# Value products as float32 column halves in runs of eight, unsplit q and k in two of four attention groups, and one VectorE step in a third

## The chip, the cores and the metric

The kernel runs on one core of one Trainium2 chip. The metric is the device time of one execution in microseconds; 2697.52 us is the median of three runs before the change. The core's engines are named as in the profile: PE is TensorE (matmuls; PEld its weight loads), DVE is VectorE, ACT is ScalarE, POOL is GpSimd and SP is the engine whose queue issues nearly all DMAs.

## The reference

The reference is a bidirectional encoder trunk of two layers over 1024 tokens and 1024 features, float32 throughout:

```
for l in range(DEPTH):                                   # 2 layers
    h = rms_norm(x, norm1_g[l])
    proj = h @ w_in[l]                                   # columns of four head groups
    (a_cq, a_ckv, a_kr, b_q, b_k, b_v, c_q, c_k, c_v, d_q, d_k, d_v) = jnp.split(proj, splits, axis=-1)
    y_a = mla_mixer(...)      # A: 4 heads, latent q and k of 64 + 32, values of 64, dense
    y_b = diff_mixer(...)     # B: 4 heads, two softmaxes of 32 each: w = p[0] - lam * p[1], values of 64, dense
    y_c = swa_mixer(...)      # C: 4 q heads on 2 kv heads of 64, +-128 window with a sink logit
    y_d = na_mixer(...)       # D: 4 heads of 64, neighbourhood on the 64-wide grid with a bias
    mix = jnp.concatenate([rms_norm(y_a, ...), y_b, rms_norm(y_c, ...), rms_norm(y_d, ...)], axis=-1)
    x = x + mix @ w_out[l]
    h = rms_norm(x, norm2_g[l])
    x = x + jnp.square(jax.nn.relu(h @ w_up[l])) @ w_down[l]
return rms_norm(x, final_norm_g)
```

## The kernel before

Everything lies with features on the partitions and tokens on the free axis. A float32 operand of a matmul is split into a high and a low part in the type float32r (`split`, L192: ACT copies the high part, DVE or POOL subtracts it to get the low one), and a product is then made of float32r matmuls on these parts. For the projections there are three such passes (`passes`, L219). The MLP works with seven products of half blocks in place of eight.

Each layer runs its attention groups in the order B, D, C, A. `weave` (L545) takes one step of an attention group at a time and puts in steps of other work, the *fill*: the latent projections and D's projections beside B, C's projections and the latent up-projections beside D, the first part of the output projection beside C and A. The framework then schedules the instructions of each engine by a planner of its own, in which priority and estimated times count, so that the order on PE is not the order of the code.

Every projection result goes through DRAM on its way to attention. It is evacuated with its norm or rotary factors, split into two parts (`emit_parts`, L582; `to_parts`, L629; `to_values`, L635) and stored; the attention group loads it back into stacked tiles of 128 partitions. In D, for each head, q's high part and low part lie one above the other in one tile, k's high part lies twice in a second tile, and k's low part twice in a third (L1045 to L1050), and two float32r matmuls with a contraction of 128 rows give the scores. C does the same. The values of a head are 128 columns wide: 64 of the high part and 64 of the low part.

In the dense groups B and A (`dense`, L818) four steps per group of two query tiles each make four PE transpositions of the probabilities into one PSUM bank (`step`, L842), ACT and DVE split them into `pth` and `ptl`, and one step later PE multiplies them with the values (`product`, L826): four float32r matmuls of 256 columns a step, sixteen per group. The upper and the lower 64 output rows are added in `pv_out` (L749). B makes its combined probabilities with a scaled copy on ACT (L898) and an addition on POOL (through L190).

In the banded groups D and C (`banded`, L966) one block of 128 queries sees up to three blocks of 128 keys. `score` (L973) makes a block's scores, `finish` reduces, adds mask or bias and exponentiates, `parts` (L986) transposes and splits, `apply` (L998) multiplies with the values. One head is worked at a time, with scores four blocks ahead. The row sums' reciprocals are sent through DRAM to be spread over the partitions (`denominators`, L761; `rows_of`, L269; `spread`, L284).

Of the kernel before, what the change touches and what calls it, by code (L numbers as in the profile page):

```python
# [21 lines left out]
P = 128  # L22
# [78 lines left out]
def layout(i):  # L101

    def padded(a, axis):
# [9 lines left out]
    wo = i["w_out"].reshape(n, 8, P, DM)[:, [2, 3, 6, 7, 4, 5, 0, 1]].reshape(n, DM, DM)  # L113
# [23 lines left out]
        + [col(i["out_g_" + s]) for s in ("mla", "swa", "na")]  # L137
# [10 lines left out]
class Trunk:  # L148
    def __init__(self, ctx, tc, d, out):
        self.ctx, self.tc, self.nc, self.d, self.out = ctx, tc, tc.nc, d, out  # L150
        self.ahead, self.tails = 4, deque()
        pool = lambda **k: ctx.enter_context(tc.tile_pool(**k))
        self.const = pool(name="const", bufs=1)
        self.xp = pool(name="xp", bufs=8)
        self.big = pool(name="big", bufs=16)
        self.wp = pool(name="wp", bufs=3)
        self.cp = pool(name="cols", bufs=2)
        self.dram = pool(name="dram", bufs=1, space=bass.MemoryType.DRAM)
# [110 lines left out]
    def rows_of(self, col, grid=False):  # L269
# [7 lines left out]
        if grid:  # L277
            flat = dr.rearrange("a b -> (a b)").rearrange("(r b c) -> b r c", r=16, b=8)
            self.store(flat, sb.rearrange("b (r c) -> b r c", r=16))
        else:  # L280
            self.store(dr, sb)
# [99 lines left out]
    def attention(self, l):  # L381
# [8 lines left out]
        qb, kb, vb = dr([2, 2, 4, 16, 2, S], "qb"), dr([2, 2, 4, 16, 2, S], "kb"), dr([4, P, 8, P], "vb")  # L390
        qd, kd, vd = dr([2, 2, P, S], "qd"), dr([2, 2, P, S], "kd"), dr([4, P, 8, P], "vd")
        qc, kc, vc = dr([2, 2, 2, 32, 2, S], "qc"), dr([2, 2, 32, 2, S], "kc"), dr([2, P, 8, P], "vc")
        lat, krd = dr([2, 3, P, S], "lat"), dr([2, 16, 2, S], "krd")
        qa = dr([2, 2, P, S], "qan"), dr([2, 4, 16, 2, S], "qar")
        ka, va = dr([2, 2, P, S], "kan"), dr([4, P, 8, P], "va")
# [13 lines left out]
        def proj_d():  # L409
            for t in range(2):  # L410
                yield from one(T_DQ[t], xs, self.ev_grid(rb, self.to_parts(qd[:, t], 0.125)))
                yield from one(T_DK[t], xs, self.ev_grid(rb, self.to_parts(kd[:, t])))
                yield from one(T_DV[t], xs, self.ev_grid(rb, self.to_values(vd[2 * t:2 * t + 2])))

        def proj_c():
            tabs = self.table("64", rb, nc.gpsimd)
            for t in range(2):
                yield from one(T_CQ2[t], xs, self.ev_rope(tabs, qc[:, t]))
            yield from one(T_CK, xs, self.ev_rope(tabs, kc))
# [4 lines left out]
        with ExitStack() as stack, ExitStack() as att:  # L424
            self.ap = att.enter_context(sbuf("att"))
            with self.banks(mm=2, tr=2, sb=3, pv=1):
                with sbuf("proj", "right") as self.pp:
# [37 lines left out]
                    self.weave(self.attn_d(l, qd, kd, vd, y["d"]), fill, self.RD, self.LD, every=self.EV[1])  # L465
                gout = lambda n: self.gout[n][:, l]
# [123 lines left out]
    def ev_rope(self, tabs, dst):  # L590

        dst = dst.rearrange("a g f h s -> a (g f) h s")

        def ev(n, ps):
# [7 lines left out]
            self.emit_parts(t1, [(dst[:, :, h, sl].rearrange("a p s -> p a s"), slice(h * 64, h * 64 + 64))  # L602
                                 for h in range(2)])
# [30 lines left out]

    def to_values(self, dst, tag="mm"):  # L635
# [3 lines left out]
        def then(n, y):  # L639
# [3 lines left out]
            src = ps.rearrange("p (k h d) -> p h k d", k=4, h=2)  # L643
            b = self.both()
            v = b.rearrange("p h (k e) -> p h k e", k=4)
            nc.scalar.activation(v[..., 0:64], src, AF.Copy)
            self.tt(v[..., 64:128], src, v.bitcast(F)[..., 0:64], ALU.subtract)
            self.keep(dst[:, :, n * 4:n * 4 + 4].rearrange("h p k e -> p h (k e)"), b.bitcast(F))
# [100 lines left out]
    def pv_out(self, pv, y, j, half, grid=False):  # L749

        t = self.ap.tile([P, 512], R, tag="ptl", bufs=3, name="pvt").bitcast(F)[0:64]
        self.nc.scalar.activation(t, pv[64:128], AF.Copy)
        a, b, o = pv[0:64], t, y[j * 64:(j + 1) * 64]
        if grid:
            a, b = (v.rearrange("p (b r c) -> p b r c", b=4, r=16) for v in (a, b))
            o = o.rearrange("p (r b c) -> p b r c", b=8, c=8)[:, 4 * half:4 * half + 4]
        else:
            o = o[:, half * 512:half * 512 + 512]
        self.tt(o, a, b, ALU.add)

    def denominators(self, z, dst, grid=False):  # L761
        r = self.col("rz", 8)
# [3 lines left out]
        self.spread(dst, rows)  # L766
# [26 lines left out]
    def vtile(self, src):  # L793
        v = self.ap.tile([P, 8, P], R, tag="v", bufs=2, name="v")
        self.load(v.bitcast(F), src)
# [22 lines left out]
    def dense(self, heads):  # L818
# [5 lines left out]
        ready = []  # L824

        def product(job, j, h, lo):  # L826
            probs, g, v, y, half, done = job
            if g % 2 == 0 and j == 0:
                self.pv = self.bank("pv")
            out = self.pv[:, (g % 2) * 256:(g % 2) * 256 + 256]  # L830
            for k in range(2):
                kt = j * 2 + k
                sl = slice(k * 256, k * 256 + 256)
                nc.tensor.matmul(out, v[:, kt], h[:, sl], start=kt == 0, stop=False)  # L834
                nc.tensor.matmul(out, v[:, kt], lo[:, sl], start=False, stop=kt == 7)  # L835
            if j == 3:
                if g % 2:
                    self.pv_out(self.pv, y, half, g // 2)
                if g == 3:
                    done()  # L840

        def step(job, j):  # L842
# [5 lines left out]
            h, lo = self.transposed(512)  # L848
            self.split(h, lo, t)
            ready.append((job, j, h, lo))  # L850
            if len(ready) > 1:
                product(*ready.pop(0))
# [15 lines left out]
        product(*ready.pop(0))  # L868
        yield True

    def attn_b(self, l, t, qb, kb, vb, out):
# [3 lines left out]
        def head(h2):  # L875
# [15 lines left out]
            def probs(qt):  # L891
# [6 lines left out]
                nc.scalar.activation(ps[1], ps[1], AF.Copy, scale=c)  # L898
                self.tt(ps[0], ps[0], ps[1], ALU.add, nc.gpsimd)
# [66 lines left out]
    def banded(self, qs, ks, v, y, j, finish, grid=False):  # L966
# [4 lines left out]
        tiles, pair = {}, {}  # L971

        def score(i):  # L973
            if i % 2 == 0:
                pair["p"] = self.ptile()
            at = i % 2 * 512
            lo, hi = max(i - 1, 0), min(i + 1, 7)
            keys = slice(lo * P, (hi + 1) * P)
            s0, w = at + (lo - i + 1) * P, (hi - lo + 1) * P
            ps = self.bank("sb")[:, :w]  # L980
            for n, k in enumerate(ks):
                mm(ps, qs[:, i * P:(i + 1) * P], k[:, keys], start=n == 0, stop=n == 1)
            tiles[i] = pair["p"][:, at:at + 384]
            finish(ps, pair["p"][:, s0:s0 + w], i)

        def parts(kb):  # L986

            t = self.bank("tr")
            i0, i1 = max(kb - 1, 0), min(kb + 1, 7)
            for i in range(i0, i1 + 1):  # L990
                nc.tensor.transpose(t[:, (i - i0) * P:(i - i0 + 1) * P],
                                    tiles[i][:, (kb - i + 1) * P:(kb - i + 2) * P], self.ident)
            w = (i1 - i0 + 1) * P
            h, l = self.transposed(w)
            self.split(h, l, t[:, :w])
            return h, l, i0, i1

        def apply(pv, half, kb, part):  # L998
            h, l, i0, i1 = part
            q0, q1 = max(i0, half * 4), min(i1, half * 4 + 3) + 1  # L1000
            src = slice((q0 - i0) * P, (q1 - i0) * P)
            dst = pv[:, (q0 - half * 4) * P:(q1 - half * 4) * P]
            mm(dst, v[:, kb], h[:, src], start=False, stop=False)
            mm(dst, v[:, kb], l[:, src], start=False, stop=kb == 4 + 3 * half)
# [4 lines left out]
        pv = self.zeroed()  # L1009
        held = []  # L1010
        for kb in range(8):
            if kb + self.ahead < 8:
                score(kb + self.ahead)
            part = parts(kb)
            if kb in (3, 4):
                held.append(part)
            if kb <= 4:
                apply(pv, 0, kb, part)
            else:
                apply(pv, 1, kb, part)  # L1020
            if kb == 4:
                self.pv_out(pv, y, j, 0, grid)
                pv = self.zeroed()
                for i, p in enumerate(held):
                    apply(pv, 1, 3 + i, p)
            yield True
        self.pv_out(pv, y, j, 1, grid)

    def zeroed(self):

        pv = self.bank("pv")
        self.nc.tensor.matmul(pv, self.zero, self.zero[:, 0:1].broadcast_to([P, 512]), start=True, stop=False)
        return pv

    def attn_d(self, l, qd, kd, vd, ys):
        nc = self.nc
        for t in range(2):
            y, rz = self.ypair(), self.rz_tile()
            for h2 in range(2):
                h = 2 * t + h2  # L1040
                bias = self.ap.tile([P, 6, P], F, tag="bias", bufs=1, name="bias")
                self.load(bias, self.d["bias"][l, h])
                qs, ks = self.stack(), [self.stack() for _ in range(2)]
                rows = slice(h2 * 64, (h2 + 1) * 64)
# [454 lines left out]
```

## Time and profile before

| | us |
|---|---|
| median of three runs (2692.25 to 2699.81) | 2697.52 |
| profiled execution | 2692.41 |
| its span on the core | 2690.6 |
| PE, sum of matmul times (95% of the span) | 2545.8 |
| DVE busy (75%) | 2014.2 |
| ACT busy (54%) | 1442.9 |
| POOL busy (18%) | 496.9 |

The granted TensorE clock was 0.971 on average. The DMA engines moved 389.15 MB. In the first layer B runs from about 85 to 330 us, D to 415, C to 480, A to 630, the rest of the output projection to 705 and the MLP to 1350; in the second B starts at about 1414, D at 1651, C at 1735, A at 1804, and A ends at 1960. In the profile's rows a group is given by line, engine, operation, the tile written and the tiles read; then come count, busy time, the mean time of one in ns, and the engine's idle time before them with what ended it. A line is often that of a helper, such as L190 for any two-operand step and L196 for any rounded copy.

### The profile page before, as it was taken

How to read it: one execution, taken by the hardware profiler on the slowest of the kernel's cores; microseconds unless marked ns; L12 is line 12 of the kernel's file. 1: busy time of each engine (PE TensorE's matmuls, PEld its weight loads, DVE VectorE, ACT ScalarE, POOL GpSimd, SP SyncE). 2: the span in 40 equal slices, each digit the busy share in tenths (PEclk: the TensorE clock that was granted, in tenths of full speed). 3: DMA queues.
4: the chain of work that ended last, by engine and by line, in shares of the span. 5: the costliest groups of instructions: out<-in, count | busy, mean ns of one | idle time of the engine just before them, and what ended most of it. 6: DMA issues, size and time to landing. Idle time of an engine off the chain costs nothing.

```text
span 2690.6 us, 36835 instructions
## 1 busy us (share of the span) xinstructions
PE 2545.8 (95%) x12296; PEld 2107.6 (78%) x12296; DVE 2014.2 (75%) x3827; ACT 1442.9 (54%) x2601; POOL 496.9 (18%) x306
## 2 busy tenths in 40 slices
PE   8989988999899999999999999789998999999997
PEld 7778876787778887888877788678887788778886
DVE  6777867774977778888668777677749677788886
ACT  4667757664534444444437777576635344444444
POOL 2555642201000000000035556331010000000000
PEclk9999989999999999999999999889999999999998
DMA  5533598322144447444244446962221444664431
GB/s 169 177 106 123 160 282 254 83 88 60 51 154 143 161 162 269 146 141 141 96 136 140 121 118 174 306 200 70 70 71 61 152 152 151 227 221 150 132 102 63
DMA packets 186927, 389.15 MB, mean 145 GB/s; under 512 B 23712, under 2 KB 26736, under 8 KB 186736
## 3 DMA queue, kind: packets, MB, share of 16 engines
q1 hardware_dynamic: 172912, 361.62, 43.7%
q10 hardware_dynamic: 13824, 25.17, 2.6%
q8 instruction: 97, 1.59, 0.2%
q14 instruction: 94, 0.77, 0.1%
HBM read 263.29 MB, written 123.41 MB: 144 GB/s over the span
## 4 chain that ended last, share of the span: by engine, by line
PE 74%; DVE 12%; DMA 6%; ACT 4%; issue 3%; POOL 1%; SPq 0%; DVEq 0%; ACTq 0%; POOLq 0%
PE u L222 8%; PE u L224 8%; PE u L223 8%; PE mm L222 5%; PE mm L223 5%; PE mm L224 5%; PE p L222 5%; PE p L223 5%; PE p L224 5%; PE sb L810 3%; PE tr L846 2%; DVE p L812 2%; DVE part L190 2%; PE pv L835 2%; PE pv L834 2%
## 5 line engine op out<-in xcount | busy, mean ns | idle before, releaser
L196 ACT ACTIVATE wh<-raw 128x512 fp32r<-128x512 f32 x448 | 281.8, 630 | 595.9 <-PE u L223 336.0
L190 DVE TENSOR_TENSOR wl<-raw,wh 128x512 fp32r<-128x512 f32 x448 | 306.8, 685 | 76.9 <-ACT wh L196 75.6
L190 POOL TENSOR_TENSOR wl<-ws,wh 128x512 fp32r<-128x512 f32 (+1 forms) x112 | 146.5, 1310 | 1107.0 <-DMA saved<-x 664.1
L224 PE MATMUL u<-far,wl 128*128 128x512 f32 x768 | 302.4, 394 | 6.2 <-DVE wl L190 6.0
L222 PE MATMUL u<-far,wh 128*128 128x512 f32 x768 | 302.4, 394 | 3.3 <-ACT ev L1251 2.1
L223 PE MATMUL u<-far,wh 128*128 128x512 f32 x768 | 301.8, 393 | 0.9 <-DVE far L190 0.9
L190 DVE TENSOR_TENSOR ptl<-tr,pth 128x512 fp32r<-128x512 f32 (+2 forms) x384 | 238.3, 629 | 67.5 <-ACT pth L196 65.8
L815 ACT ACTIVATE p<-p,nm 128x1024 f32<-128x1024 f32 x192 | 220.1, 1147 | 91.1 <-DVE nm L812 89.6
L196 ACT ACTIVATE pth<-tr 128x512 fp32r<-128x512 f32 (+2 forms) x384 | 204.9, 546 | 104.4 <-PE tr L846 55.8
L222 PE MATMUL p<-far,wh 128*128 128x512 f32 x640 | 251.2, 393 | 2.6 <-DVE ev L190 2.6
L224 PE MATMUL p<-far,wl 128*128 128x512 f32 x640 | 250.0, 391 | 2.9 <-DVE wl L190 2.9
L223 PE MATMUL p<-far,wh 128*128 128x512 f32 x640 | 250.3, 391 | 0.0
L810 PE MATMUL sb<-stack 96*128 96x512 f32 x640 | 217.6, 421 | 18.8 <-DVE nm L812 17.8
L190 POOL TENSOR_TENSOR p<-p 128x1024 f32<-128x1024 f32 x64 | 154.0, 2410 | 141.4 <-ACT p L898 132.1
L190 DVE TENSOR_TENSOR raw<-raw 128x512 f32<-128x512 f32 x256 | 174.6, 686 | 6.7 <-DMA raw<-in_w_up 2.0
L224 PEld LDWEIGHTS u<-far,wl 128*128 128x128 f32 x768 | 145.8, 190 | 38.4 <-DVE wl L190 7.9
L222 PEld LDWEIGHTS u<-far,wh 128*128 128x128 f32 x768 | 146.1, 190 | 35.3 <-ACT ev L1251 2.9
L223 PEld LDWEIGHTS u<-far,wh 128*128 128x128 f32 x768 | 145.8, 190 | 31.9 <-DVE far L190 1.6
L222 PE MATMUL mm<-xh,wh 128*128 128x512 f32 x416 | 168.9, 406 | 1.3 <-DVE part L190 0.7
L812 DVE CUSTOM_DVE_ANT_0 p<-sb,zero,nm 128x512 f32<-128x512 f32 x192 | 142.4, 742 | 32.2 <-PE sb L810 28.6
L224 PE MATMUL mm<-xh,wl 128*128 128x512 f32 x416 | 166.5, 400 | 0.0
L223 PE MATMUL mm<-xl,wh 128*128 128x512 f32 x416 | 166.4, 400 | 0.0
(245 smaller groups left out, 5993.1 us busy)
## 6 DMA issues: line engine op xcount, KB each, us to landing
act<-acts SPq DMA_DIRECT2D x224, 256.0 KB
raw<-in_w_up SPq DMA_DIRECT2D x128, 256.0 KB
acts<-ev SPq DMA_DIRECT2D x128, 256.0 KB
raw<-in_w_down SPq DMA_DIRECT2D x128, 256.0 KB
acts<-ev ACTq DMA_DIRECT2D x96, 256.0 KB
ws<-in_w_in SPq DMA_DIRECT2D x76, 256.0 KB
rz<-drows SPq DMA_DIRECT2D x40, 256.0 KB
stack<-kd SPq DMA_DIRECT2D x32, 256.0 KB
```

Of the source, the lines that this page charges most:

```text
L190: (eng or self.nc.vector).tensor_tensor(out=out, in0=a, in1=b, op=op)
L196: nc.scalar.activation(hi, src, AF.Copy)
L222: mm(ps, w[0], x[0][:, sl], start=start, stop=False)
L223: mm(ps, w[0], x[1][:, sl], start=False, stop=False)
L224: mm(ps, w[1], x[0][:, sl], start=False, stop=stop)
L810: self.nc.tensor.matmul(ps, q[:, qt * P:(qt + 1) * P], k[:, sl], start=i == 0, stop=i == len(passes) - 1)
L812: self.nc.vector.tensor_tensor_reduce(out=p[:, sl], in0=ps, in1=self.zero[:, 0:1].bitcast(F).broadcast_to([P, 512]), scale=-scale, scalar= ...
L815: self.nc.scalar.activation(p, p, AF.Exp, bias=nm[:, 1:2], scale=-1.0, accum_out=z)
L834: nc.tensor.matmul(out, v[:, kt], h[:, sl], start=kt == 0, stop=False)
L835: nc.tensor.matmul(out, v[:, kt], lo[:, sl], start=False, stop=kt == 7)
L846: nc.tensor.transpose(t[:, k * 256 + i * P:k * 256 + (i + 1) * P], p[:, (j * 2 + k) * P:(j * 2 + k + 1) * P], self.ident)
```

## The change

- Value products (A, B, C, D): the transposed probabilities are copied once in float32 (`pt`), by ACT in B and D, by DVE and ACT in turn in C and A. The values are float32 and 64 columns wide. In A and B two successive key tiles go to PSUM partitions 0 to 63 and 64 to 127, in a run of eight matmuls per group, issued two steps into the next group; `pv_out` adds the two halves as before. In C and D the two halves are two heads, so nothing is added (`pair_out`).
- Scores of D and C: q and k are stored and loaded as they are, two heads in one tile of 128 partitions, and the score of a head is one float32 matmul with a contraction of the 64 rows of its half. The two heads of a pair are worked together, with scores three blocks ahead. In C a pair is the two kv heads with the same q index, and the rows of the output weights and of the gain are reordered for it. Bias and mask lie in tiles of the pool of `stack` (L743).
- B: the two exponentiated tiles are combined by one VectorE instruction in place of the copy on ACT and the addition on POOL.

The core of the diff:

```diff
-        self.ahead, self.tails = 4, deque()
+        self.ahead, self.tails = 3, deque()
...
-                yield from one(T_DQ[t], xs, self.ev_grid(rb, self.to_parts(qd[:, t], 0.125)))
-                yield from one(T_DK[t], xs, self.ev_grid(rb, self.to_parts(kd[:, t])))
+                yield from one(T_DQ[t], xs, self.ev_grid(rb, self.to_rows(qd[t], 0.125)))
+                yield from one(T_DK[t], xs, self.ev_grid(rb, self.to_rows(kd[t])))
...
+            self.turns = (False, False)
...
+                self.turns = (True, False)
...
+    def to_rows(self, dst, scale=None):
+
+        def then(n, y):
+            if scale is not None:
+                self.nc.scalar.activation(y, y, AF.Copy, scale=scale)
+            self.keep(dst[:, n * 512:n * 512 + 512], y)
+        return then
...
-    def transposed(self, w):
-
-        return [self.ap.tile([P, 512], R, tag=n, bufs=3, name=n)[:, :w] for n in ("pth", "ptl")]
+    def transposed(self, ps):
+
+        t = self.ap.tile([P, 512], F, tag="pt", bufs=self.NT, name="pt")[:, :ps.shape[1]]
+        if self.turns[0]:
+            self.nc.vector.tensor_copy(t, ps)
+        else:
+            self.nc.scalar.activation(t, ps, AF.Copy)
+        self.turns = self.turns[::-1]
+        return t
...
+        def products():
+            job, pts = runs.pop(0)
+            probs, g, v, y, half, done = job
+            if g % 2 == 0:
+                self.pv = self.bank("pv")
+            out = self.pv[:, (g % 2) * 256:(g % 2) * 256 + 256]
+            for n, j in enumerate((3, 2, 1, 0)):
+                for k in range(2):
+                    nc.tensor.matmul(out[k * 64:(k + 1) * 64], v[:, j * 2 + k], pts[j][:, k * 256:k * 256 + 256],
+                                     start=n == 0, stop=n == 3)
...
                     if job:
                         step(job, 2 * i)
                         step(job, 2 * i + 1)
+                    if i == 0 and runs:
+                        products()
...
-                nc.scalar.activation(ps[1], ps[1], AF.Copy, scale=c)
-                self.tt(ps[0], ps[0], ps[1], ALU.add, nc.gpsimd)
+                nc.vector.scalar_tensor_tensor(out=ps[0], in0=ps[1], scalar=c, in1=ps[0], op0=ALU.mult, op1=ALU.add)
...
-            for n, k in enumerate(ks):
-                mm(ps, qs[:, i * P:(i + 1) * P], k[:, keys], start=n == 0, stop=n == 1)
+            ps = [self.bank("sb")[:, :w] for _ in heads]
+            for b, r in zip(ps, heads):
+                mm(b, q[r, i * P:(i + 1) * P], k[r, lo * P:(hi + 1) * P], start=True, stop=True)
...
+        def products(pv, half, kbs):
+            for kb in kbs:
+                pts, i0, i1 = done[kb]
+                q0, q1 = max(i0, half * 4), min(i1, half * 4 + 3) + 1
+                for r, v, pt in zip(heads, vs, pts):
+                    mm(pv[r, (q0 - half * 4) * P:(q1 - half * 4) * P], v[:, kb], pt[:, (q0 - i0) * P:(q1 - i0) * P],
+                       start=False, stop=kb == 2 + 3 * half)
```

More of the change, by code (lines that the diff above doesn't have):

```diff
@@ L765, in denominators @@
         yield
-        self.spread(dst, rows)
+        for j in range(n):
+            self.spread(dst[j * 64:(j + 1) * 64] if n > 1 else dst, rows, j, n)
         yield
@@ L823, in dense @@
         nc = self.nc
[L824 to L840, printed above, removed]
+        ready, runs = [], []
         def step(job, j):
@@ L847, in step @@
                                         p[:, (j * 2 + k) * P:(j * 2 + k + 1) * P], self.ident)
[L848 to L852, printed above, removed]
+            ready.append(self.transposed(t))
+            if j == 3:
+                runs.append((job, list(ready)))
+                ready.clear()
+        def products():
[8 more added lines that the diff above has]
+                                     start=n == 0, stop=n == 3)
+            if g % 2:
+                self.pv_out(self.pv, y, half, g // 2)
+            if g == 3:
+                done()
         job = None
@@ L867, in dense @@
             step(job, j)
-        product(*ready.pop(0))
+        while runs:
+            products()
         yield True
@@ L986, in parts @@
         def parts(kb):
-            t = self.bank("tr")
             i0, i1 = max(kb - 1, 0), min(kb + 1, 7)
[L990 to L1004, printed above, removed]
+            out = []
@@ new lines, in parts, with zeroed @@
+            for j in range(2):
+                t = self.bank("tr")
+                for i in range(i0, i1 + 1):
+                    at = j * 512 + (kb - i + 1) * P
+                    nc.tensor.transpose(t[:, (i - i0) * P:(i - i0 + 1) * P], tiles[i][:, at:at + P], self.ident)
+                out.append(self.transposed(t[:, :(i1 - i0 + 1) * P]))
+            done[kb] = out, i0, i1
+        def zeroed():
+            pv = self.bank("pv")
+            mm(pv, self.zero, self.zero[:, 0:1].broadcast_to([P, 512]), start=True, stop=False)
+            return pv
@@ new lines, in attn_d, with finish @@
+            biases = []
+            for j in range(2):
+                b = self.stack(F)[:, 0:768].rearrange("p (a b) -> p a b", a=6)
+                self.load(b, self.d["bias"][l, 2 * t + j])
+                biases.append(b)
+            q, k = self.stack(F), self.stack(F)
+            self.load(q, qd[t])
+            self.load(k, kd[t])
+            vs = [self.vtile(vd[2 * t + j]) for j in range(2)]
+            z = self.col("zz", 16)
+            def finish(j, ps, p, i):
+                b0 = {0: 4, 7: 3}.get(i, 0)
+                w = ps.shape[1]
+                nm = self.col("nb")
+                nc.vector.tensor_tensor_reduce(
+                    out=p, in0=ps, in1=biases[j][:, b0:b0 + w // P].rearrange("p a b -> p (a b)"),
+                    scale=-1.0, scalar=3e38, op0=ALU.add, op1=ALU.min, accum_out=nm)
+                nc.scalar.activation(p, p, AF.Exp, bias=nm, scale=-1.0, accum_out=z[:, j * 8 + i:j * 8 + i + 1])
@@ L1065, in attn_d @@
+            yield from self.banded(q, k, vs, y, finish, True)
+            self.tails.append(self.denominators(z, rz, 2))
             self.tails.append(self.times(y, rz))
```

193 lines of the change are left out of this document (84 added, 109 removed).

## The prediction, made before the changed kernel was run

> **What bounds the kernel now.** I read the page first, then the busy times by stage, then the chain of waits inside each attention stage.
>
> ```profile
> span 2690.6 us, 36835 instructions
> PE 2545.8 (95%) x12296; PEld 2107.6 (78%) x12296; DVE 2014.2 (75%) x3827; ACT 1442.9 (54%) x2601; POOL 496.9 (18%) x306
> ```
>
> The 95% of PE is no rate: a matmul's recorded time runs on beside the next one's. The rate is in the starts (first column; the second is the duration):
>
> ```profile
> 562.81 0.28 PE L835 MATMUL pv<-ptl,v 128*128 128x256 f32 x1
> 562.93 0.28 PE L834 MATMUL pv<-pth,v 128*128 128x256 f32 x1
> 563.76 0.60 PE L846 MATMUL tr<-ident,p 128*128 128x128 f32 x4
> 701.14 0.39 PE L223 MATMUL u<-opl,wh 128*128 128x512 f32 x1
> 701.37 0.39 PE L224 MATMUL u<-oph,wl 128*128 128x512 f32 x1
> ...
> 35.76 1.95 PE L299 MATMUL mm<-ident,rs_r 128*128 128x128 f32 x16
> 454.63 1.95 PE L265 MATMUL mm<-ones,sq 128*128 128x1 f32 x16 [1.78 <-DVE sq L190]
> ```
>
> So a float32r matmul of 512 columns costs 0.227 us (mean step of many; here 0.23), of 256 columns 0.12, of 384 about 0.17 (three quarters of 0.227). A float32 transposition of 128 columns costs (0.60 - 0.272)/3 = 0.109. A plain float32 matmul is recorded as two instructions: the sixteen of L299 are eight in the code. Now the stages, with these prices on every record (B, D, C, A, output projection, MLP of layer 0; then B, D, C, A of layer 1):
>
> ```profile
> core 0: us, PE busy (x) PEld busy (x) DVE busy (x) ACT busy (x) POOL busy (x), PEclk, DMA share, GB/s
> 85.00:330.00 245.00, 233.29 (x1230) 194.76 (x1229) 189.22 (x473) 175.65 (x285) 140.29 (x80) 0.96 0.43 128
> 330.00:415.00 85.00, 74.72 (x401) 63.58 (x400) 55.32 (x143) 53.33 (x132) 36.63 (x24) 0.90 0.97 287
> 415.00:480.00 65.00, 54.90 (x290) 42.17 (x288) 48.52 (x129) 45.36 (x118) 18.68 (x11) 0.95 0.72 224
> 480.00:630.00 150.00, 141.93 (x875) 121.05 (x874) 110.06 (x247) 96.13 (x172) 13.70 (x10) 1.00 0.24 69
> 705.00:1350.00 645.00, 627.76 (x2734) 515.63 (x2735) 508.15 (x790) 292.49 (x488) 4.81 (x3) 0.99 0.47 151
> 1414.00:1651.00 237.00, 226.95 (x1208) 189.90 (x1206) 183.04 (x467) 174.26 (x283) 138.40 (x78) 0.97 0.43 125
> 1651.00:1735.00 84.00, 73.55 (x410) 63.93 (x407) 54.50 (x140) 52.07 (x130) 38.73 (x26) 0.94 0.97 281
> 1735.00:1804.00 69.00, 55.70 (x280) 44.67 (x281) 50.01 (x129) 45.91 (x119) 17.45 (x10) 0.83 0.75 237
> 1804.00:1960.00 156.00, 147.99 (x897) 126.02 (x897) 116.72 (x255) 98.73 (x179) 16.01 (x10) 0.99 0.25 70
> ```
>
> The groups by line add up to what PE's stream needs. Here are the first row of each stage's list, with D's last (20 groups in D, 17 in C, 14 in A, 13 in B):
>
> ```profile
> L982 PE MATMUL sb<-stack 128*128 128x384 f32 (+1 forms) x70 | 18.6, 383 | 2.9 <-DVE nb L1058 2.9
> ...
> L273 PE MATMUL mm<-ident,rz 128*8 128x128 f32 x1 | 0.3, 272 | 0.0
> ...
> L982 PE MATMUL sb<-stack 128*128 128x384 f32 (+1 forms) x58 | 15.2, 368 | 2.2 <-DVE nb L1089 2.0
> ...
> L810 PE MATMUL sb<-stack 96*128 96x512 f32 x189 | 53.6, 407 | 2.5 <-DVE nm L812 2.3 <-DVE nb L1089 0.2
> ...
> L222 PE MATMUL mm<-xh,wh 128*128 128x512 f32 x185 | 75.7, 409 | 0.2 <-DVE both L190 0.2
> ```
>
> Counts times prices give 214 us of PE need in B's 245 (0.87), 61 in D's 85 (0.72), 41 in C's 65 (0.63) and 128 in A's 150 (0.85). The MLP, almost all 512-column matmuls, needs 2734 x 0.227 = 621 of 645, 0.96: I take that as full. So B and A have some slack on PE, D and C much. Who holds D shows in its chain, whose longest pieces are all transfers, on DMA engines that are 97% busy:
>
> ```profile
> 352.27 9.05 DMA stack<-kd
> 361.39 9.95 DMA latp<-lat
> 371.41 8.90 DMA vc<-both
> ...
> 411.63 8.38 DMA mask<-in_swa
> ```
>
> **What the change takes off D, C and their DMA.** One wait on the bias (us in total, times, longest) and the loads of q and k, all in D's window:
>
> ```profile
> DVE p L1058 <- DMA bias<-in_bias: 9.4, 3, 6.6
> ...
> stack<-kd SPq DMA_DIRECT2D x10, 256.0 KB
> stack<-kc SPq DMA_DIRECT2D x8, 256.0 KB
> stack<-qc SPq DMA_DIRECT2D x8, 256.0 KB
> stack<-qd SPq DMA_DIRECT2D x4, 256.0 KB
> ```
>
> A D pair loads 24 x 256 KB a layer now and 4 x 512 KB after, a third: 3.67 MB here become 1.2. C's sixteen (4.2 MB) become three of 512 KB (1.6). That is 5.1 MB less; stores of q, k, v halve (vc, kc, va: about 1.5 MB), v tiles halve (about 0.8). Some 7.4 MB of 85 us x 287 GB/s = 24.4 MB go, which at 287 GB/s is 26 us: D's transfers then need about 59 of 85 us. Each store leaves SP's queue with its DVE or POOL split, so what stands behind a store there moves up too. The biases also get tiles of their own, where one buffer now makes DVE wait for the load, 9.4 us in D. So transfers stop being last; PE comes next, unless DVE does. DVE loses its part of the split (ptl, 0.685 us for 512 columns, row below) and the two-half additions, so it falls from 55 and 49.
>
> **What it does to DVE, ACT, POOL in B and A.** Whole-run rows:
>
> ```profile
> L190 DVE TENSOR_TENSOR ptl<-tr,pth 128x512 fp32r<-128x512 f32 x256 | 173.2, 685 | 43.0 <-ACT pth L196 42.2
> L196 ACT ACTIVATE pth<-tr 128x512 fp32r<-128x512 f32 x256 | 148.0, 590 | 59.5 <-PE tr L846 55.8 <-DVE ptl L190 1.8 <-PE pv L834 0.2
> L898 ACT ACTIVATE p<-p,cb 128x1024 f32<-128x1024 f32 x64 | 72.9, 1144 | 12.2 <-DVE cb L897 10.3 <-DVE cb L896 0.8 <-DVE rs_r L255 0.7
> L190 POOL TENSOR_TENSOR p<-p 128x1024 f32<-128x1024 f32 x64 | 154.0, 2410 | 141.4 <-ACT p L898 132.1
> L190 DVE TENSOR_TENSOR y<-y,rz 128x1024 f32<-128x1024 f32 x8 | 10.8, 1366 | 21.6 <-DMA rz<-drows 21.6
> ```
>
> Per layer in B: DVE loses 64 x 0.685 = 44 us and gains 32 one-step combinations; the trace has none of this form, the nearest is the 1.366 us addition of the same size: 44 us, so DVE stays near 189. ACT loses 36 us, POOL 77, and a p tile is ready 1.14 + 2.41 - 1.37 = 2.2 us sooner. In A half of the copies go to DVE: 32 x about 0.6 = 19 in place of 44, so DVE falls to 85 of 150 and ACT by 19. None of these engines ends B or A today, so this pays only up to PE's need.
>
> **What it costs PE.** Matmuls on 64 columns or 64 rows, in float32. One recorded instruction of 256 columns takes T. Ends: 0.12 (the float32r price) and 0.218 (twice the transposition's 0.109, the one float32 stream in the trace that columns bind; L299 and L265 take 1.95 us for sixteen whether 128 columns or 1, so their weights bind). I take 0.218, the same data type. [...]
>
> - A and B: 64 runs of eight, each 16 x 0.12 = 1.92 before and 9 x 0.218 + 0.32 = 2.28 after; in the compiled issue order 47 of these stand whole, the others are broken by scores or transpositions into some 30 more pieces, each 0.218 + 0.32. Together +39 us, 10 per stage. If T were 0.12 it would be -22.
> - D and C scores: 128 matmuls of K = 64 where 256 were. The issue order has only 20 pairs and 8 triples together, and 64 alone, and a lone one has nothing beside it: 64 x (2 x 0.327 + 0.32) + 20 x (3 x 0.327 + 0.32) + 8 x (4 x 0.327 + 0.32) = 101 us, less 6 for the narrow end blocks, against 192 x 0.17 + 64 x 0.12 = 40. So +55.
> - D and C products: 160 matmuls in 56 pieces, mean T 0.24: 216 x 0.24 + 56 x 0.32 = 70 against about 41, and 16 fewer zeroing matmuls (0.23 each): +25. With the scores that is 20 per stage.
>
> A run also waits as a whole for its fourth copy; behind it on PE stand scores and projection, and DVE waits for those. It is issued two transposition steps later, and a copy is 0.59 us, so I price this at nothing; uncovered it is 64 x 0.59 = 38 us.
>
> **The sum.** Need over 0.96: B (214 + 10)/0.96 = 233 for 245; A (128 + 10)/0.96 = 144 for 150; D (61 + 20)/0.96 = 84 for 85; C (41 + 20)/0.96 = 64 for 65. That is 20 us a layer, 40 in all; layer 1 has the same stages within a few us (237, 84, 69, 156). Setup, output projection and MLP are not touched. The profiled execution took 2692.4 us (span 2690.6), the median is 2697.5: 5 us above it, so 2657 is the forecast on the median.
>
> **The rivals.**
> - Slower: the halves do not overlap in float32. For it: nothing in this trace ever ran two tiles together. [...] Then runs take 16 x 0.218 (+130 in A and B), scores +66, products +50: B 257, A 167, D 94, C 73 by the same division, +46 a layer, about 2790. It decides from the point where a run of eight takes over 2.9 us with its switches (2.28 and 40 x 0.96/64 = 0.6). Chance 0.20.
> - The switches cost more, 0.28 at each edge (the 256-column matmul's whole time): 242 x 2 x 0.12 = 58 us more on PE, 60 with the division, so 2717. The gain is gone at 0.24 an edge. Chance 0.14.
> - The switches cost nothing: B 225, A 136, D 72, C 51: over 100 us faster, near 2575 (DVE or DMA may stop it at about 2610). Chance 0.16.
> - PE isn't what is next: D, C and A keep their length by the exp, copy and product steps one behind another, and the change cannot be told from none (2690 to 2705). For it: A's chain has DVE and ACT steps between the matmuls. Chance 0.08.
>
> **How the numbers follow.** The forecast has 0.42, with its own range 2630 to 2685. Eight in ten: from 2600 (part of the free switches) to 2775 (serial halves in part hidden by slack). What a measurement of this kernel can tell is about 0.3%, 8 us: faster 0.58, same 0.09, slower 0.33.
>
> **What would show it.** Right: in a run, the second half's starts fall beside the first's, eight products take about 2 us, D's DMA share is well under 0.97 and its chain is PE; A's DVE falls to some 85 us. Wrong: eight products over 2.9 us, or idle PE before and after each run of over 0.24 us; or D as long as before with its transfers short.

## The result and the profile after

The changed kernel takes 2715.91 us (median of four runs, 2711.66 to 2717.93), the kernel before 2698.22: a ratio of 1.0068, interval 1.0047 to 1.0088. It is slower by 0.7% where I had forecast 1.5% faster. The profiled execution took 2717.18 us, its span is 2715.4.

The busy times on the page after show that the change did to the engines what was asked of it. DVE lost 127 us, ACT 132, POOL 173, and PE's weight loads 109; only PE's own matmuls did not get fewer us.

```profile
span 2715.4 us, 35525 instructions
...
PE 2592.6 (95%) x12272; PEld 1998.4 (74%) x12272; DVE 1886.9 (69%) x3515; ACT 1310.9 (48%) x2405; POOL 324.1 (12%) x222
```

The busy times by stage (B, D, C, A and the output projection of layer 0, then C and the output projection of layer 1), columns as in the prediction:

```profile
85.00:317.00 232.00, 224.07 (x1165) 168.39 (x1164) 179.08 (x430) 142.20 (x250) 56.22 (x37) 0.96 0.36 104
317.00:400.00 83.00, 83.00 (x397) 51.02 (x395) 30.90 (x89) 41.97 (x110) 22.18 (x15) 1.00 0.52 144
400.00:478.00 78.00, 71.25 (x326) 40.35 (x322) 40.48 (x110) 43.82 (x116) 26.10 (x18) 0.87 0.67 213
478.00:630.00 152.00, 150.15 (x897) 108.81 (x897) 87.88 (x204) 77.38 (x137) 20.71 (x12) 0.98 0.24 69
630.00:714.00 84.00, 70.02 (x301) 56.92 (x300) 35.73 (x54) 25.49 (x45) 12.41 (x11) 0.92 0.23 73
1751.00:1817.00 66.00, 63.42 (x295) 34.20 (x295) 37.03 (x96) 42.17 (x109) 23.56 (x16) 0.95 0.72 224
1963.00:2050.00 87.00, 73.91 (x317) 59.45 (x314) 37.53 (x56) 26.26 (x46) 12.09 (x11) 0.90 0.22 64
```

The row of the kernel before for its output projection, which the prediction leaves out:

```profile
630.00:695.00 65.00, 64.99 (x294) 53.25 (x293) 34.06 (x50) 24.41 (x44) 12.72 (x11) 1.00 0.27 82
```

Two rows stand out. The output projection, which has the same matmuls in both kernels, had PE busy all the time before; after, it takes some 19 us more, 14 of them with PE idle, at a granted clock of 0.92. And C of layer 0 is long, at a clock of 0.87. D is as forecast: DMA share 0.52 in place of 0.97, and PE fills it.

For all kernels below I measured the stages alike: B from its fourth score matmul (the first ones stand some 20 us ahead of the rest), D and A from their first, C from VectorE's first step on its scores (in the kernel before C's first scores stand 13 us ahead of it, waiting for the mask), A up to its last value product, and the output projection from there to the MLP's first matmul (us, layer 0 / layer 1; the sums are of the unrounded times):

| kernel | B | D | C | A | B to A together | output projection |
|---|---|---|---|---|---|---|
| before | 239 / 231 | 90 / 91 | 56 / 63 | 151 / 154 | 536 / 537 | 68 / 68 |
| changed | 226 / 227 | 82 / 86 | 79 / 66 | 148 / 146 | 535 / 525 | 86 / 87 |
| B's step undone (e9) | 229 / 229 | 83 / 83 | 55 / 54 | 149 / 150 | 515 / 516 | 85 / 85 |
| and nine steps left at A (e12) | 228 / 228 | 84 / 84 | 59 / 60 | 154 / 154 | 524 / 524 | 68 / 69 |

The MLP takes 640 to 643 us and, up to the end of the span, 663 to 666 in all of them. The experiments ran in several sittings, in which the median of the kernel before was 2697.8 to 2700.2, so differences across them are good to some 2 us. So the loss is in two places: 37 us in the two output projections, and, seen against e9, 30 us in the attention stages.

### The profile page after: what moved, and what is told of

Same layout as the page of the kernel before. It is cut to its first block, busy times and chain, and to the rows that moved or that the text cites. A ratio compares the mean times of both kernels' runs of the same rounds, so it can differ in the third digit from the quotient of the medians.

```text
span 2715.4 us, 35525 instructions
## 1 busy us (share of the span) xinstructions
PE 2592.6 (95%) x12272; PEld 1998.4 (74%) x12272; DVE 1886.9 (69%) x3515; ACT 1310.9 (48%) x2405; POOL 324.1 (12%) x222
## 5 line engine op out<-in xcount | busy, mean ns | idle before, releaser
L227 PE MATMUL u<-far,wl 128*128 128x512 f32 x768 | 302.0, 393 | 6.2 <-DVE wl L193 6.0
L225 PE MATMUL u<-far,wh 128*128 128x512 f32 x768 | 302.8, 394 | 4.1 <-ACT ev L1270 2.1
L225 PE MATMUL p<-far,wh 128*128 128x512 f32 x640 | 250.9, 392 | 2.5 <-DVE ev L193 2.5
L227 PE MATMUL p<-far,wl 128*128 128x512 f32 x640 | 249.5, 390 | 2.7 <-DVE wl L193 2.7
L826 ACT ACTIVATE pt<-tr 128x512 f32<-128x512 f32 (+2 forms) x288 | 151.0, 547 | 125.9 <-PE tr L860 62.6
L227 PEld LDWEIGHTS u<-far,wl 128*128 128x128 f32 x768 | 145.9, 190 | 38.2 <-DVE wl L193 7.9
L225 PEld LDWEIGHTS u<-far,wh 128*128 128x128 f32 x768 | 145.9, 190 | 37.0 <-ACT ev L1270 2.9
L225 PE MATMUL mm<-xh,wh 128*128 128x512 f32 x416 | 169.4, 407 | 0.1
L227 PE MATMUL mm<-xh,wl 128*128 128x512 f32 x416 | 168.2, 404 | 0.0
L860 PE MATMUL tr<-ident,p 128*128 128x128 f32 x1024 | 154.5, 276 | 9.2 <-ACT pt L826 5.5
L840 PEld LDWEIGHTS sb<-stack 96*128 96x128 f32 x640 | 115.6, 193 | 60.1 <-DVE nm L842 21.8
```

Source lines behind the costliest of these rows:

```text
L225: mm(ps, w[0], x[0][:, sl], start=start, stop=False)
L227: mm(ps, w[1], x[0][:, sl], start=False, stop=stop)
L826: self.nc.scalar.activation(t, ps, AF.Copy)
L840: self.nc.tensor.matmul(ps, q[:, qt * P:(qt + 1) * P], k[:, sl], start=i == 0, stop=i == len(passes) - 1)
L860: nc.tensor.transpose(t[:, k * 256 + i * P:k * 256 + (i + 1) * P], p[:, (j * 2 + k) * P:(j * 2 + k + 1) * P], self.ident)
```

## The experiments

**Where the output projection's 19 us come from.** What the weaving loop calls after each step of an attention group is `tick`: it serves *one* step of the waiting work, in order (row sums through DRAM, multiplications by their reciprocals, norms).

```
    def tick(self):
        while self.tails:
            if next(self.tails[0], self) is not self:
                return
            self.tails.popleft()
```

How often it is called for each attention step is set by `EV = (.5, .5, .7, 1)` for B, D, C and A, which the change leaves alone. But with two heads worked together, D and C have 20 steps a layer and not 36. They now serve 10 and 14 waiting steps and not 18 and 25; with B's 9 that is 33 of 52 where it was 52 of 60, so 19 are left when A starts, more than the 17 that A serves, where it was 8. VectorE's timeline shows what this does after A's last product at 628. Each `rows<-mm` is one head's row sums on their way to DRAM, and the last one the factors of A's norm; the number in brackets is the idle time before.

```profile
629.54 0.28 DVE L278 COPY rows<-mm 8x128 f32<-8x128 f32 x1
636.62 0.28 DVE L278 COPY rows<-mm 8x128 f32<-8x128 f32 x1 [6.80 <-PE mm L276]
642.32 1.23 DVE L193 TENSOR_TENSOR y<-y,rz 128x1024 f32<-128x1024 f32 x1 [5.41 <-DMA rz<-drows]
647.66 0.28 DVE L278 COPY rows<-mm 8x128 f32<-8x128 f32 x1 [4.12 <-PE mm L276]
655.97 0.28 DVE L278 COPY rows<-mm 8x128 f32<-8x128 f32 x1 [8.03 <-PE mm L276]
663.47 1.23 DVE L193 TENSOR_TENSOR y<-y,rz 128x1024 f32<-128x1024 f32 x1 [7.22 <-DMA rz<-drows]
...
672.55 0.28 DVE L278 COPY rows<-mm 8x128 f32<-8x128 f32 x1 [0.55 <-PE mm L276]
```

The same in the kernel before, where A's last product ends at 627:

```profile
631.76 0.28 DVE L275 COPY rows<-mm 8x128 f32<-8x128 f32 x1 [2.91 <-PE mm L273]
...
654.17 0.28 DVE L275 COPY rows<-mm 8x128 f32<-8x128 f32 x1 [3.21 <-PE mm L273]
```

Before, one head's row sums and the norm's remain; after, four heads' go through DRAM one behind another, and the norm, which must wait for them, comes 18 us later. The rival reason is that the value products now come one group later, which delays A's last row sums by itself. e1 gives D and C the rates for 18 and 25 steps and changes nothing else; e2 takes the rates down in the kernel before.

```diff
-    EV = (.5, .5, .7, 1)
+    EV = (.5, .9, 1.26, 1)      # e1, on the changed kernel
+    EV = (.5, .28, .39, 1)      # e2, on the kernel before
```

> The changed kernel with one line altered: EV = (.5, .9, 1.26, 1). Theory (late tails): the change takes D's and C's attention steps from 36 to 20 a layer, and one waiting tail step (row sums, norms, mixing) is served for every so many steps, so some 19 tail steps are left when A begins and all four of A's denominators are sent to DRAM and back after A's last product. The new rates give D 18 and C 25 tail steps again. Then three of the four denominators lie inside A, the output projection goes back from 84 and 85 us to about 66, and the time falls by 30 to 40 us to about 2680, below the 2698 of the kernel before. Rival 1 (the tails are late because a head's products, and with them its denominators, come one group later): two or more denominators still stand after A, and under 10 us are gained. Rival 2 (PE is the bound and the work only moves): attention grows by what the output projection loses, 2710 to 2720.

> The kernel before with EV = (.5, .28, .39, 1), so that its D and C serve 10 and 14 tail steps, as the changed kernel does. Theory (late tails): about 20 us longer output projection in each layer, some 2730, with the four denominators of A after A's last product. Rival 1 (products one group later are what delays them): nearly unchanged, 2698 to 2705.

e1: 2689.39 us, 0.9968 of the kernel before (0.9952 to 0.9983), output projection 69 / 69. e2: 2783.69 us (1.031, 1.0293 to 1.0327), output projection 92 / 95, and C 83 / 93 for 56 / 63. The late steps are shown in both directions; the later products are not the reason, for e1 keeps them. Neither time is quite the expected one. e1's gain of 26.5 us is less than the 35 that the output projection gave back: A is longer there, 163 / 157. e2 loses 84 us where I expected some 32: its four attention stages are longer too, by 19 and 29 us, C above all.

**B's one VectorE step**, by itself on the kernel before (e4), and undone in the changed kernel (e9) and in e1 (e8):

```diff
-                nc.scalar.activation(ps[1], ps[1], AF.Copy, scale=c)
-                self.tt(ps[0], ps[0], ps[1], ALU.add, nc.gpsimd)
+                nc.vector.scalar_tensor_tensor(out=ps[0], in0=ps[1], scalar=c, in1=ps[0], op0=ALU.mult, op1=ALU.add)
```

> The kernel before with only B's combination made in one VectorE step. DVE swaps nothing here (its low-part subtractions stay), so it gains 32 x about 1.37 = 44 us a layer in B on top of 189 of 245, near full; ACT loses 37 us and POOL 77. Theory A (PE sets B, and the p tiles come sooner): -5 to +5 us. Rival (DVE becomes the bound of B): +10 to +40 us.

> The changed kernel with the tail rates of e1_ticks and B's combination on ACT and POOL as before. In e4_b_step_only the one VectorE step alone cost about 15 us, as DVE was full in B. Theory: with the split gone from DVE, B's DVE here is 172 - 44 = 128 of 224 us and ACT 137 + 37 = 174, so both have room and PE stays the bound: within 5 us of e1_ticks (2689). Rival (the combination was what the sooner p tiles of B were worth): 10 us or more above e1_ticks.

> The changed kernel with B's scaled copy on ScalarE and addition on GpSimd back in place of the one VectorE step; the rates of waiting steps as the change left them. Theory (late row sums and the VectorE step are two costs that add): the step gave 15.8 us with the rates set right (2689.4 to 2673.7), so about 2700 here, no more than 2705, with B some 6 to 8 us shorter a layer and the output projection still 86 us a layer. Rival (the step costs only because of where waiting steps then fall): 2710 to 2716, the output projection shorter and B as long as before.

e4: 2713.97 us (1.0062, 1.0039 to 1.0084), so +14.5 on its batch, as its rival had it. e8: 2673.65 (0.990, 0.9874 to 0.9926), 15.7 under e1, where the theory had at most 5 either way and the rival a loss. e9: 2683.32 (0.9941, 0.9921 to 0.9961), 32.6 under the changed kernel: neither theory had that, for the two costs do not add (33 and 26.5 singly, 42 together). In all three pairs the kernel with the VectorE step loses, and so it does in a fourth (e6 against e11, below). The group of the step after, ACT's longest wait in B (100 to 310 us) before and after, and the same wait in e9:

```profile
L929 DVE SCALAR_TENSOR_TENSOR p<-p,cb 128x1024 f32<-128x1024 f32 x64 | 87.6, 1368 | 1.3
```

```profile
ACT p L815 <- DVE nm L812: 24.5, 18, 4.3
```

```profile
ACT p L845 <- DVE nm L842: 51.6, 39, 3.0
```

```profile
ACT p L845 <- DVE nm L842: 23.1, 19, 3.0
```

The step takes what I had assumed, 1.368 us. But it shares VectorE with the row maxima that ScalarE's exponentials wait for, and that wait doubles against e9; in 13 of the 39 waits, 22 us of them, the step itself runs on VectorE during the wait. That this wait is how the step costs its time is argued and not shown: in e4 it rises only from 24.5 to 32.1 us, and ScalarE, which has lost the scaled copy, has more time to wait. B itself gets no longer by the step (226 for 229): the planner leaves fill undone there, which D and then C take over. The rows count D's projection matmuls that run in D's window. A product is a triple of matmuls, one in each of L222 to L224 (L225 to L227 after), and one of the three nearly equal rows is shown for each kernel: before, changed, e9.

```profile
L224 PE MATMUL mm<-xh,wl 128*128 128x512 f32 x24 | 10.1, 421 | 0.0
```

```profile
L227 PE MATMUL mm<-xh,wl 128*128 128x512 f32 x47 | 19.1, 407 | 0.0
```

```profile
L227 PE MATMUL mm<-xh,wl 128*128 128x512 f32 x35 | 14.0, 400 | 0.0
```

With the step 12 more triples fall into D (12 x 3 x 0.227 = 8 us), and D, full on PE, passes other work on to C. There PE meets what is not ready; the waits on PE in C (400 to 480 us) of the changed kernel, and C of e9:

```profile
PE mm L661 <- ACT part L663: 3.2, 1, 3.2
PE mm L661 <- DVE part L193: 1.7, 2, 1.4
PE mm L744 <- DMA latp<-lat: 1.1, 1, 1.1
```

```profile
404.00:459.00 55.00, 54.03 (x271) 28.97 (x270) 32.78 (x92) 38.25 (x101) 19.70 (x13) 1.00 0.80 252
```

Of the 25 us that C of layer 0 is longer than in e9, about 8 are matmuls moved in (3 triples of L225 to L227, 7 products of L744, 32 records of L268, which belong to norms), 6 are PE idle, and 11 are the clock (0.86 of 80 us against 1.00). Why the planner orders B's fill so is not shown.

**The parts by themselves.** e6 is the kernel before with A's and B's value products of the change and with the VectorE step; e11 is e6 without the step; e7 is e1 with A and B (their products and the combination) as before. In short:

```diff
+ e6:  dense(): products() in runs of eight, one float32 copy; B's step; D, C, EV as before
+ e11: e6 with B's scaled copy and addition back
+ e7:  D and C of the change, EV (.5, .9, 1.26, 1); dense() and B as before
```

> Only A's and B's part of the change, with D and C of the kernel before and the old tail rates, which fit them: float32 value products in column halves in runs of eight, and B's combination in one VectorE step. Fewer buffers for copies (6, shared with the parts of D and C) than the changed kernel has (8), for space. Theory: a run takes 8 x 0.213 + 0.2 = 1.9 us of PE as before (16 x 0.12), and B gains from a DVE with the split taken off: B falls by some 10 us a layer as in e1_ticks, 2675 to 2690. Rival (what e1_ticks won came from the lighter transfers in D and C): 2695 to 2705.

> Only D's and C's part of the change, with the tail rates of e1_ticks and with A and B of the kernel before (7 buffers for the copies). Theory: D's DMA share falls from 0.97 to about 0.5 to 0.6 and its chain turns to PE, whose lone float32 scores and tile switches take what the transfers gave: D and C together stay within 5 us a layer of before, the time at 2690 to 2710. Rival (transfers were the bound and PE has room): D and C lose 10 us or more a layer, 2670 to 2680.

> The kernel before with the float32 column halves in runs of eight in A and B alone; B's combination in two steps, D and C and the rates as before. If the parts add, it is the run with the VectorE step (2717.1, before 2697.8) less what that step costs alone (14.5 to 16): 2701 to 2703, no change. If the halves are worth in this kernel what they are worth beside the new D and C (2673.7 against 2697.5, 24 us), it is about 2675.

e6: 2717.14 (1.0062, 1.004 to 1.0084), above both ranges. e7: 2697.51 (0.9984, 0.9965 to 1.0003), in its theory's range. e11: 2711.1 (1.0041, 1.0029 to 1.0053), a miss for both theories. So the new D and C by themselves change nothing, the column halves in A and B cost 11 us (with six buffers for copies in e11, and not eight, which no run separates), and both together gain 24 (e8). D and C of e11 point to the reason:

```profile
320.00:418.00 98.00, 84.75 (x449) 70.69 (x447) 54.21 (x141) 54.61 (x134) 44.12 (x31) 0.91 0.92 255
418.00:491.00 73.00, 59.43 (x290) 48.33 (x291) 48.50 (x127) 44.85 (x116) 20.21 (x12) 0.84 0.61 189
```

```profile
L224 PE MATMUL mm<-xh,wl 128*128 128x512 f32 x43 | 17.1, 397 | 0.0
```

In layer 0 B is shorter here too, 227 for 239, and here too D has 43 projection triples for 24 before: 19 x 3 x 0.227 = 13 us of work, as much as B lost. B did not get faster; work left it. (In layer 1 B keeps its 231, and D has 37 triples for 32.) The old D, at a DMA share of 0.92, cannot take the work in (98 / 93 us, clock 0.91); the new D can, at a clock of 1.00. By this reading, which fits e7, e8 and e11 but which no run tests by itself, the room in D is what the change is worth.

**Do the halves run beside each other?** e3 issues all four matmuls of the first half and then the four of the second.

```diff
-            for n, j in enumerate((3, 2, 1, 0)):
-                for k in range(2):
+            for k in range(2):
+                for n, j in enumerate((3, 2, 1, 0)):
```

> The changed kernel with the loops of a run of eight exchanged: four products of the lower 64 columns first, then four of the upper. If the halves run beside each other in the changed kernel (its trace has their starts 7 ns apart and 0.21 us per pair and pass), each run here takes about 16 x 0.213 + 0.2 = 3.6 us and not 1.9, 64 runs add about 109 us of PE work in A and B, and the time rises by 70 to 110 us to 2785 to 2825. If they do not overlap in truth and only the recorded starts do, a run stays near 1.9 us and the time near 2716.

2774.61 us (one run, so without an interval), 58.7 over the changed kernel: fewer than expected. A run of eight on PE's timeline in the changed kernel, and in e3:

```profile
618.15 1.95 PE L875 MATMUL pv<-pt,v 128*64 128x256 f32 x16
620.03 1.09 PE L860 MATMUL tr<-ident,p 128*128 128x128 f32 x8
```

```profile
613.08 2.86 PE L875 MATMUL pv<-pt,v 128*64 128x256 f32 x16
```

Sixteen instructions take 1.95 us together and 2.86 in turn, where I expected 3.6: 0.91 us more is some four steps of 0.216 us, so by this estimate half of the sixteen still have one of the other half beside them. 64 x 0.91 = 58 us is the whole difference measured. In the 47 whole runs of the changed kernel the two halves start 6 to 8 ns apart, and inside a run the pairs follow in steps of 0.216 us (median; the first step of a run is 0.26 to 0.27).

**Are the lone scores dear?** e5 is e1 with the two heads' score matmuls of a block held together.

```diff
-            for b, r in zip(ps, heads):
-                mm(b, q[r, i * P:(i + 1) * P], k[r, lo * P:(hi + 1) * P], start=True, stop=True)
+            with self.tc.tile_critical():
+                for b, r in zip(ps, heads):
+                    mm(b, q[r, i * P:(i + 1) * P], k[r, lo * P:(hi + 1) * P], start=True, stop=True)
```

> The changed kernel with the tail rates of e1_ticks and each pair of score matmuls of D and C kept together in PE's order (64 pairs; in e1_ticks 52 of the 128 stand alone, 23 pairs and 10 triples are together). A lone one takes two passes of 0.32 us and a switch of about 0.1 at each edge, a pair no more than that, 0.85 us, since both halves run together. Theory (lone scores cost PE, and PE bounds D and C): about 24 groups fewer, 24 x 0.85 = 20 us of PE work less, so 10 to 20 us below e1_ticks, about 2675. Rival (the pairs wait for the later of two PSUM banks, and PE's order was not what D and C wait for): within 5 us of e1_ticks, or above it.

2741.61 us (1.0151, 1.0121 to 1.018), 52 above e1, D 106 / 103 for 83 / 88. The theory is wrong, but that does not price the lone score: held together, the pair waits for things it doesn't read, such as this one in D (waits on PE, 320 to 426 us):

```profile
PE sb L1011 <- DMA latp<-lat: 6.4, 1, 6.4
```

So the price of a lone score stays open.

**How early should the waiting work be?** e10 is e8 with higher rates, e12 e8 with lower ones.

```diff
-    EV = (.5, .9, 1.26, 1)      # e8: none left at A's start
+    EV = (.5, 1, 1.6, 1)        # e10: none left, and earlier
+    EV = (.5, .7, 1.02, 1)      # e12: nine left
```

> The version with the right rates and B's old two steps, with still higher rates in D and C: EV (.5, 1, 1.6, 1) in place of (.5, .9, 1.26, 1), so that C leaves no waiting step to A. Theory (what counts is only that A's own reciprocals are not queued behind others when A ends): the same as with the lower rates, 2668 to 2682, output projection 68 or 69 us a layer. Rival (every step taken earlier gains): under 2665. Second rival (in C the steps get in the way of attention): over 2685, C over 70 us in both layers.

> The version with B's old two steps, with rates of (.5, .7, 1.02, 1): D then serves 14 and C 20 waiting steps a layer, so that 9 are left when A starts (8 in the kernel before, none with .9 and 1.26, 19 as the change left it). Theory (the row sums of A must not queue behind others, but a waiting step served in C costs time there): output projection 68 to 70 us a layer, C 54 to 60 us as with the rates unchanged, so 2683 less two times 16 plus a little in A: 2652 to 2668. Rival (a waiting step costs the same wherever it stands inside the attention stages): no better than with .9 and 1.26, 2670 to 2683, C or A longer by 8 us or more a layer than in the kernel with the rates unchanged.

e10: 2699.24 (0.9999, 0.9985 to 1.0014); e12: 2672.97 (0.991, 0.9893 to 0.9926), as good as e8: these two are the fastest here, 24 and 26 us under the kernel before. Against e9 the output projection of e12 gives back 17 us a layer, and the attention stages, C and A, take about 9 of them: the time is the rival's, though neither C nor A alone is longer by the 8 us that it named. e10 has the time of its second rival, but not the place: C is 68 / 66, the output projection is no better than in e8, and A is 163 / 164 for 149 / 152. In A of layer 0 there is a norm's wait (waits on PE, 505 to 530 us) and the clock that follows. PE idles 4 us more than in e8 and the clock takes 4; the other 6 of these 14 us were not traced.

```profile
PE mm L268 <- DVE sq L193: 2.4, 1, 2.4
```

```profile
513.00:523.00 10.00, 7.65 (x43) 5.95 (x44) 4.97 (x13) 4.96 (x10) 1.91 (x1) 0.79 0.65 157
523.00:533.00 10.00, 10.00 (x50) 7.47 (x47) 5.12 (x13) 4.20 (x7) 0.67 (x1) 0.87 0.10 35
```

## Why the prediction was wrong, point by point

- **"Setup, output projection and MLP are not touched"** is the step that failed: for the output projection the sum has a term of nothing. The matmuls there are the same, but the work they wait for is paced by the steps of D and C, and the change takes 16 of 36 of these away in each. I had counted instructions, and not how often the weaving loop calls `tick`. The term measured 37 us, of the 59 by which the forecast was missed (2657 for 2716).
- **"DVE stays near 189 ... None of these engines ends B"**: the busy times were right (179 of 232), the price of nothing was not: 33 us by e9, 14.5 alone by e4. VectorE's share of 0.77 does not tell what one more step on it costs the engine that waits for its results; how it costs is only in part shown, see above.
- **The run of eight**: 2.28 forecast, 1.92 before. From the end of one transposition's stream to the start of the next, a run takes 1.97 us. T is 0.216, as assumed (0.218). No run shows the ninth T of the sum, nor the 0.32 us, 0.16 an edge, that it gives every piece (the switches of the rivals): the first instructions of both halves start 6 to 8 ns apart, so that a run takes 8 T, and n matmuls n T for an even n; and the two edges add 0.24 us to 8 T. So the edges do cost time, but little. For the 47 runs that stand whole, as many as forecast, +0.36 us was +0.05. The other 17 stand in 47 pieces, and a piece of an odd number of matmuls has one with nothing beside it; by the starts of all pieces the +39 us were about 20.
- **Need over 0.96**: the rule itself did not hold in the attention stages, and what fills a stage did not stay there. In layer 0, 11 (e9) to 23 (changed) projection triples left B for D, 8 to 16 us, and A took over seven triples of the output projection from C, 5 us. With these and 5 us a stage for the runs I count some 203 to 212 us of need in B's 226 to 229 and 138 in A's 148 to 149: 0.90 to 0.93, where the MLP had 0.96. That the four stages are together 21 and 22 us a layer shorter in e9, where my sum had 20, is luck: B and A give 12 and 5 where the sum had 18, with B's part moved work, and D and C give 9 and 17 where it had 2.
- **D**: 84 forecast, 82 / 86 measured, and the bound is as forecast: PE fills the stage and the DMA share is 0.52. The transfers fell further than I had it, from 24.4 MB to 12 (144 GB/s for 83 us) and not to 17. The time is right in part by luck: in layer 0, 23 projection triples more ran in D and some 34 matmuls on `latp` fewer, a net 8 us of fill that the sum did not have, so the +20 for D's scores and products was too high by an estimated 8 us. (The 24 loads of 256 KB in the working are D's four heads and not one pair; the bytes are right.)
- **The smaller terms**: A's DVE: 85 forecast, 87.9 measured. The run that waits for its fourth copy, priced at nothing: PE's idle time before products in A is 0.7 us, right. The side sum for T = 0.12 comes to -20 by its own terms, not -22; nothing hangs on it.
- **The rivals**: serial halves are refuted by e3, where a run with less overlap takes 2.86 us for 1.95. Dear switches are refuted by the 0.24 us of both edges; that this rival's 2717 is the measured time is an accident. Free switches come nearer to the price of a run, yet their 2575 is far off, so the price of the switches does not decide this kernel's time. "No change" describes only the D and C part (e7). None named a wait outside the four stages.

## What to carry to other kernels

Where a step counter paces other work, a change that alters the number of steps moves that work, and the place to look is the stage where it is waited for, not the one that was edited. A stage that gets shorter has won only if the next one did not receive its instructions: count one matmul by stage in both traces. And moving a step onto an engine with room still needs the question who is waiting behind it in that engine's queue.

## What the hardware showed that I had not expected

The clock is a term of its own in these comparisons. Span times (1 - granted clock) gives the time lost to it, as a mean over the runs: 78 us before, 79 changed, 88 in e11, 66 in e1, 64 in e9 and e10, 52 in e8, 50 in e12, 125 in e2. Of the 15.7 us between e1 and e8, 14 are clock. In the profiles of the kernel before and of the changed one the granted clock is 0.50 in 27 and in 19 stretches, of 3.41 us or a multiple of it (up to 17.07; the last of each runs on past the end of the span), so 1.7 us are lost in each 3.41. Ahead of 44 of the 46, PE was idle in one piece of 1.2 to 4.7 us within the last 7. But the clock also falls with PE recorded as busy throughout: here e8's PE timeline, and the busy times of the microseconds around it.

```profile
362.04 1.72 PE L268 MATMUL mm<-pairs,rz 128*128 128x2 f32 x14
```

```profile
363.00:364.00 1.00, 1.00 (x11) 1.00 (x12) 0.03 (x1) 0.00 (x0) 0.00 (x0) 1.00 0.99 221
364.00:365.00 1.00, 1.00 (x6) 0.81 (x5) 0.81 (x5) 0.76 (x3) 0.00 (x0) 0.58 1.11 250
365.00:366.00 1.00, 1.00 (x5) 0.89 (x4) 0.11 (x1) 0.99 (x6) 0.00 (x0) 0.50 0.98 221
366.00:367.00 1.00, 1.00 (x3) 0.73 (x3) 0.35 (x2) 0.58 (x2) 0.00 (x0) 0.50 1.09 246
367.00:368.00 1.00, 1.00 (x5) 0.79 (x4) 0.00 (x0) 0.00 (x0) 0.00 (x0) 0.71 0.99 221
368.00:369.00 1.00, 1.00 (x6) 0.84 (x5) 0.00 (x0) 0.00 (x0) 0.00 (x0) 1.00 0.25 53
```

Matmuls of one or two columns, as the norms use, come just before it, fourteen records in 1.72 us here; no run varied them. The changed kernel's C in layer 0 has such a case too: the clock falls to 0.50 at 470.87 us, for 13.65 us, with PE recorded as busy for all of the 7 us before it, behind the row below. So about 7 of the 11 us of clock there follow waits, and 4 follow the norm's matmuls.

```profile
468.94 1.62 PE L268 MATMUL mm<-ones,sq 128*128 128x1 f32 x14
```
